# Hybrid decoder layer on one core: the down projection in seven products per pair, with its sums formed during the up projection and kept in DRAM

## The chip, the core and the metric

The kernel runs on one core of one Trainium2 chip. The metric is the device time of one execution in microseconds (us). TensorE (PE) multiplies matrices into PSUM; VectorE (DVE), ScalarE (ACT) and GpSimd (POOL) work elementwise; SyncE (SP) issues most of the DMA transfers. Each engine works through its own queue in order and waits on semaphores of the others.

## The reference, cut to what matters

One layer of a decoder for 1024 tokens of width 1024, all in float32. A token-mixing half (attention in windows of 128 in parallel with a gated linear recurrence, then an output projection) is followed by a squared-ReLU MLP with 4096 hidden columns. The change touches the MLP alone:

```python
h = rmsnorm(x, pre_w_mlp[l]) * (1.0 + sc2) + sh2
u = jnp.square(jax.nn.relu(h @ w_up[l]))
x = x + g2 * rmsnorm(u @ w_down[l], post_w_mlp[l])
```

`w_up` is 1024x4096 and `w_down` is 4096x1024; `g2` comes from the conditioning vector through a slice of the matrix called `wada` in the kernel.

## The kernel before, in words

**Precision.** Every big matrix product is made in float32 from two reduced-precision halves: an operand is split into `hi` (a rounding copy on ACT) and `lo` (operand minus `hi`, on DVE), and the product is hi x hi + hi x lo + lo x hi. So one 128x128 by 128x512 block product is three matmuls, and every operand block that comes from DRAM costs one ACT and one DVE instruction of 128x512 before TensorE can use it.

**The up projection** (from line 1159 on; the loop over `p` is at line 1178). The 32 blocks of 128 hidden columns are taken in 16 pairs. The first four blocks (pairs 0 and 1, "CL") are done in the plain way by `up_cl`. For pairs 2 to 15 the product of a 2x2 arrangement (two hidden blocks by two halves of the inner dimension, against two halves of the inner dimension by two halves of the tokens) is made by Strassen's scheme in its Winograd form: seven products instead of eight, each of 12 matmuls. The token side's sums (`bt`, numbers 1 to 8, `factors` at line 994) are formed once and stay in SBUF; the weight side's sums are formed for each pair by `up_weights` (line 1041: four DVE sums, seven splits). `prod` (line 1064) issues the 12 matmuls of one product, and `up_pair` (line 1096) puts products 1, 4 (of the pair before), 5, 2, 6, 3, 7 in order. They accumulate in three PSUM banks, called `pua`, `puc`, `pub` in the profile. Between products a bank is copied out by ACT (`snap`) or added to an SBUF tile by DVE (`merge`). `act2` (line 1086) then applies ReLU on ACT and the square on POOL, and POOL issues the DMA that writes the block to the DRAM tensor `ud`. The tiles of these results (`s1`, `s5`, `s2`, `u`) come from a pool `poolM` of 16 buffers, eight of which hold the sums number 4 of the token side. Weights are loaded one to two pairs ahead by `up_loads` on SP, through pools of four (`poolR2`) and three (`poolR`) buffers.

**The down projection** (`down`, line 1199) is plain. In eight stages `s` of four hidden blocks, for each of eight token blocks `tb` and both halves of the output columns, 12 matmuls go into a fresh PSUM bank (`pd` in the profile, from a pool `pb` of five banks), and DVE adds the bank to an SBUF accumulator `acc`. While a stage runs, `load_u` and `load_wd` fetch the next stage's operands from DRAM (`ud` and `w_dn`, 16 blocks of 128x512 in a stage) on SP and split them on ACT and DVE. In stages 2 to 5 the vector `gw2` (`g2` times the output norm's weight) is computed by `modrow` (line 161): 16 loads of `wada` and 16 multiply-adds `macc` on DVE. In the last stage each token block, once finished, is normalised, scaled, added to the residual `x1` (reloaded from DRAM) and stored (`final`, line 1228); the last two blocks have code of their own (`last_two`, line 1236).

**What sets the order.** The program's text gives the order of dependences; a scheduler then places the instructions on each engine's queue by its own estimate of when they become ready, except where the text pins engines to program order (`pin`). Pools hand out buffers, and an instruction that writes a buffer waits until all readers of its former content, DMA writes among them, are done. All engine instructions go through the helper class at line 39, so profile rows name tiles rather than lines.

Of the kernel before, what the change touches and what calls it, by code (L numbers as in the profile page):

```python
# [16 lines left out]
P = 128  # L17
# [30 lines left out]
def hybrid_layer(ctx: ExitStack, tc: tile.TileContext, I, out, dbg=None):  # L48
# [963 lines left out]
    ud = dram.tile([2 * NG, 2, P, 512], F32, tag="ud", name="ud")  # L1012
# [28 lines left out]
    def up_weights(p, ns=(1, 5, 2, 6, 3, 7, 4)):  # L1041
        for n in ns:
            a11, a12, a21, a22 = (araw[p, k] for k in ("a11", "a12", "a21", "a22"))
            if n == 5:
                araw[p, "s1"] = s1 = t_(f"s1_{p}")
                DVE.tensor_tensor(s1, a21, a22, ALU.add)
                wsplit(5, p, s1)
            elif n == 6:
                araw[p, "s2"] = s2 = t_(f"s2_{p}")
                DVE.tensor_tensor(s2, araw[p, "s1"], a11, ALU.subtract)  # L1050
                wsplit(6, p, s2)
            elif n == 3:
                s4 = t_(f"s4_{p}")
                DVE.tensor_tensor(s4, a12, araw[p, "s2"], ALU.subtract)
                wsplit(3, p, s4)
# [30 lines left out]
    def act2(p, src, f, th, e=None, on_act=False):  # L1086
# [7 lines left out]
        nc.gpsimd.dma_start(ud[2 * p + f, th], e)  # L1094

    def up_pair(p):
        if (p, "a") not in banks:
            prod(p, 1)
        if (p - 1, "a") in banks:
            prod(p - 1, 4, False)  # L1100
            act2(p - 1, banks[p - 1, "a"], 1, 0)
# [5 lines left out]
        act2(p, ev[p, "s1"], 0, 0, ev[p, "s1"])  # L1107
# [10 lines left out]
    NS, SF = 8, 4  # L1118
    us, wd = {}, {}
    DPn = {}  # L1120

    def d_(name, dt=F32):
        return DPn["d"].tile([P, 512], dt, tag="d", name=name)

    def load_u(s, th, raws_=None, mk=None):
        for i, f in enumerate(range(SF * s, SF * s + SF)):
            rk = raws_[i % len(raws_)] if raws_ else raw_
            us[f, th] = split(load_raw(rk, f"ur{f}_{th}", ud[f, th]), mk or (d_ if th == 1 and f % SF else m_), f"u{f}_{th}")

    def load_wd(s, half, raws_=None):  # L1130
        for i, f in enumerate(range(SF * s, SF * s + SF)):
            rk = raws_[i % len(raws_)] if raws_ else raw_
            wd[f, half] = split(load_raw(rk, f"wdr{f}_{half}", I["w_dn"][f][:, half * 512:half * 512 + 512]),
                                hT_, f"wd{f}_{half}")
# [10 lines left out]
    def up_cl(f, th):  # L1145
# [4 lines left out]
        act2(f // 2, pst, f % 2, th, t_(f"rl{f}_{th}"), True)  # L1150
# [12 lines left out]
    R2 = uctx.enter_context(tc.tile_pool(name="poolR2", bufs=4))  # L1163
    load_cl(3)
# [12 lines left out]
    up_loads(p0 + 1)  # L1177
    for p in range(p0, NG):
        if p + 1 < NG:
            up_weights(p + 1, (1, 5, 2))  # L1180
        else:
            pin(True, SP)
            load_wd(0, 0, (raw_, t_))
            load_u(0, 0, (raw_, t_), hT_)
            load_wd(0, 1, (raw_, t_))
            pin(False, SP)
# [5 lines left out]
    prod(NG - 1, 4, False)  # L1192
    act2(NG - 1, banks[NG - 1, "a"], 1, 0)
    uctx.close()
    DPn["d"] = ctx.enter_context(tc.tile_pool(name="poolD", bufs=12))

    accs = [[None, None] for _ in range(TB)]

    def down(s, tb):
        sl = slice(tb % 4 * P, tb % 4 * P + P)  # L1200
        fs = range(SF * s, SF * s + SF)
        for half in range(2):
            pst = tp_ps(f"pd{s}_{tb}_{half}")
            proj3(pst, [tuple(u[:, sl] for u in us[f, tb // 4]) for f in fs], [wd[f, half] for f in fs])
            if s == 0:
                accs[tb][half] = g_(f"acc{tb}_{half}")
                ACT.activation(accs[tb][half], pst, AF.Copy)
            else:
                DVE.tensor_tensor(accs[tb][half], pst, accs[tb][half], ALU.add)
# [26 lines left out]
    def last_two(s, x16, x17):  # L1236
        a, b = TB - 2, TB - 1
        pin(True, ACT, DVE, POOL, PE)
        down(s, a)
        fs = range(SF * s, SF * s + SF)  # L1240
        lhs = [tuple(u[:, 3 * P:] for u in us[f, 1]) for f in fs]
        ss = small.tile([P, 3], F32, tag="ssl", bufs=1, name="ssl")
        one = {n: small.tile([P, 1], F32, tag="l_" + n, bufs=1, name="l_" + n) for n in ("part", "t", "r")}
        finl = a_ps("finl")
        cols = ((0, 512), (512, 768), (768, D))
        accl = [accs[b][c0 // 512][:, c0 % 512:c0 % 512 + c1 - c0] for c0, c1 in cols]

        def piece(n):
            c0, c1 = cols[n]
            pst = tp_ps(f"pdl{n}")[:, 0:c1 - c0]  # L1250
            half, b0 = c0 // 512, c0 % 512
            proj3(pst, lhs, [tuple(w[:, b0:b0 + c1 - c0] for w in wd[f, half]) for f in fs])
            DVE.tensor_tensor(accl[n], pst, accl[n], ALU.add)
            ACT.activation(finl[:, 0:c1 - c0], accl[n], AF.Square, accum_out=ss[:, n:n + 1])

        def gate(n):
            DVE.tensor_tensor(accl[n], accl[n], gw2[:, cols[n][0]:cols[n][1]], ALU.mult)

# [115 lines left out]
```

## Time and profile before

| | |
|---|---|
| median of 3 runs | 1166.39 us (1164.28 to 1167.32) |
| the profiled execution | 1165.2 us, its span from first to last instruction 1163.4 us |
| PE / DVE / ACT / POOL busy | 1116.1 / 690.2 / 497.6 / 315.4 us |
| DMA over the span | 132.82 MB |
| up projection, pairs 2 to 15 | about 533 to 802 us |
| down projection | 802 to 1151 us |

A group row of the profile reads: line, engine, operation, out<-in by the program's names, shape, count | busy us, mean ns of one | idle time of the engine before them and what ended it. A row of the chain of waits reads: start, length (us), what, how many instructions. A row of the timeline reads: start, length, engine, instruction, and in brackets the idle time before it with what ended that. A window row gives the busy time of each engine in a stretch with the number of instructions, then the granted clock, the busy share of the 16 DMA engines and the GB/s moved.

### The profile page before, as it was taken

Reading aid. Unit: us, or ns where it says so; the run is one execution under the profiler, and the core shown is the slowest. Engines: PE = TensorE matmul, PEld = TensorE weight load, DVE = VectorE, ACT = ScalarE, POOL = GpSimd, SP = SyncE. Lnnn points to the kernel's source line nnn. Section 1 sums busy time; section 2 is a strip of 40 time slices with the busy share of each in tenths; the row PEclk is TensorE's granted clock in tenths of the full one; section 3 lists DMA queues with packets and bytes.
Section 4 is the critical chain, followed back from the end, with each engine's and each line's share of the span. In section 5 each row is a group of like instructions: output and inputs, shape, how many; then the busy total and the mean of one; then the engine's idle time right before and its main releaser. Section 6 shows DMA issues by size and latency. Waiting matters only on the chain.

```text
span 1163.4 us, 15657 instructions
## 1 busy us (share of the span) xinstructions
PE 1116.1 (96%) x5590; PEld 914.3 (79%) x5590; DVE 690.2 (59%) x1181; ACT 497.6 (43%) x1064; POOL 315.4 (27%) x432
## 2 busy tenths in 40 slices
PE   3899999999999999999999999999999999999995
PEld 3778776788788788878788888888888888888884
DVE  4875777878765565479554545447545454454445
ACT  5454644364555655556444444435522221221122
POOL 3444221043235544422333333332000000000053
PEclk9899999999999999999999999999999999999998
DMA  9700400534311422413323323237624342333133
GB/s 336 256 10 3 144 1 22 189 98 139 110 55 44 150 106 91 150 68 104 124 106 111 117 103 123 83 118 255 216 82 127 100 124 94 99 121 98 46 109 136
DMA packets 68607, 132.82 MB, mean 114 GB/s; under 512 B 9264, under 2 KB 10032, under 8 KB 68528
## 3 DMA queue, kind: packets, MB, share of 16 engines
q1 hardware_dynamic: 61200, 108.21, 28.1%
q0 software_dynamic: 7040, 23.07, 5.1%
q8 instruction: 44, 0.72, 0.2%
q10 hardware_dynamic: 288, 0.52, 0.1%
q14 instruction: 35, 0.29, 0.1%
HBM read 106.61 MB, written 25.17 MB: 113 GB/s over the span
## 4 chain that ended last, share of the span: by engine, by line
PE 79%; DVE 7%; ACT 4%; POOL 3%; DMA 2%; issue 2%; DVEq 0%; SPq 0%; POOLq 0%; ACTq 0%
PE pd L39 29%; PE pua L39 12%; PE po L39 6%; PE puc L39 6%; PE pu L39 4%; PE pub L39 3%; PE pv L39 3%; PE pq L39 2%; PE phg L39 2%; PE phq L39 2%; PE phf L39 2%; DVE m L39 1%; PE pk L39 1%; PE sc L39 1%; PE oT L39 1%
## 5 line engine op out<-in xcount | busy, mean ns | idle before, releaser
L39 DVE TENSOR_TENSOR acc<-pd,acc 128x512 f32<-128x512 f32 x110 | 74.8, 687 | 60.6 <-PE pd L39 60.6
L39 POOL TENSOR_TENSOR s<-s 128x512 f32<-128x512 f32 x42 | 48.6, 1156 | 126.0 <-ACT s L39 126.0
L39 DVE TENSOR_TENSOR wt<-s,wt 128x512 fp32r<-128x512 f32 x42 | 29.0, 692 | 65.9 <-ACT wt L39 65.9
L39 ACT ACTIVATE wt<-a 128x512 fp32r<-128x512 f32 x56 | 35.0, 629 | 50.2 <-PE pub L39 18.6
L39 DVE TENSOR_TENSOR wt<-a,wt 128x512 fp32r<-128x512 f32 x56 | 39.2, 700 | 28.1 <-ACT wt L39 28.1
L39 DVE SCALAR_TENSOR_TENSOR macc<-wada,cs,macc 128x512 f32<-128x512 f32 x56 | 44.9, 802 | 11.9 <-DMA wada<-wada 11.2
L39 PE MATMUL pd<-wd_0l,u_0h 128*128 128x512 f32 x128 | 49.8, 389 | 0.0
L39 PE MATMUL pd<-wd_0h,u_0l 128*128 128x512 f32 x128 | 49.8, 389 | 0.0
L39 PE MATMUL pd<-wd_1h,u_0h 128*128 128x512 f32 x128 | 49.8, 389 | 0.0
L39 PE MATMUL pd<-wd_1l,u_0h 128*128 128x512 f32 x128 | 49.8, 389 | 0.0
L39 PE MATMUL pd<-wd_1h,u_0l 128*128 128x512 f32 x128 | 49.8, 389 | 0.0
L39 PE MATMUL pd<-wd_0h,u_0h 128*128 128x512 f32 x128 | 49.8, 389 | 0.0
L39 ACT ACTIVATE u_1h<-ur 128x512 fp32r<-128x512 f32 x32 | 20.0, 628 | 66.8 <-DMA ur<-ud 66.8
L39 PE MATMUL pd<-wd_0h,u_1h 128*128 128x512 f32 x124 | 48.2, 389 | 0.0
L39 PE MATMUL pd<-wd_0l,u_1h 128*128 128x512 f32 x124 | 48.2, 389 | 0.0
L39 PE MATMUL pd<-wd_0h,u_1l 128*128 128x512 f32 x124 | 48.2, 389 | 0.0
L39 PE MATMUL pd<-wd_1h,u_1h 128*128 128x512 f32 x124 | 48.2, 389 | 0.0
L39 PE MATMUL pd<-wd_1l,u_1h 128*128 128x512 f32 x124 | 48.2, 389 | 0.0
L39 PE MATMUL pd<-wd_1h,u_1l 128*128 128x512 f32 x124 | 48.2, 389 | 0.0
L39 ACT ACTIVATE wd_0h<-wdr 128x512 fp32r<-128x512 f32 x32 | 20.1, 631 | 63.4 <-PE pd L39 33.0
L39 PE MATMUL pua<-bt_0h,wt 128*128 128x512 f32 x112 | 43.8, 391 | 1.5 <-DVE s L39 1.5
L39 DVE TENSOR_TENSOR u_1l<-ur,u_1h 128x512 fp32r<-128x512 f32 x32 | 22.0, 691 | 37.0 <-ACT u_1h L39 37.0
(624 smaller groups left out, 3428.0 us busy)
## 6 DMA issues: line engine op xcount, KB each, us to landing
wada<-wada SPq DMA_DIRECT2D x64, 256.0 KB, 3.2
wdr<-w_dn SPq DMA_DIRECT2D x64, 256.0 KB, 2.9
ur<-ud SPq DMA_DIRECT2D x64, 256.0 KB, 2.7
a<-w_u SPq DMA_DIRECT2D x56, 256.0 KB, 2.8
ud<-s POOLq DMA_DIRECT2D x42, 256.0 KB, 2.7
wa<-wada SPq DMA_DIRECT2D x32, 256.0 KB, 5.2
x<-x SPq DMA_DIRECT2D x16, 256.0 KB, 4.9
xr<-x SPq DMA_DIRECT2D x16, 256.0 KB, 2.9
```

The lines of the kernel that those rows point to most:

```text
L39: ins = op(*args, **kw)
```

## The change

The down projection goes over to the same seven-product scheme, with blocks of hidden pairs as inner dimension, the two halves of the tokens on one side and the two halves of the output columns on the other.

- Up phase, activations: after the four squared blocks of a pair (`a11`, `a12`, `a21`, `a22`) DVE forms four sums of them (`usum`, numbers 7, 5, 6, 3), and seven blocks instead of four are written to `ud`. The square moves from POOL to ACT. The pairs 0 and 1 get their sums by POOL from blocks reloaded from DRAM (`direct_sums`).
- Up phase, weights: `down_sums` loads the four blocks of `w_dn` of one pair through a new pool `poolB` of three buffers, POOL forms four differences, and POOL's queue writes them to a new DRAM tensor `td`. One pair's sums are issued per iteration, from pair 0 on; in iterations 4, 5 the direct sums and in 11, 13 the last two pairs' weight sums come on top.
- `gw2` (`modrow`) moves from the down phase into iterations 6 to 9 of the up phase.
- In `up_weights` the three sums share one buffer.
- Down phase: the 16 pairs are taken in five groups (4, 4, 3, 3, 2 pairs). For the first four groups, for each of the seven products (`dstage`), four token blocks get 3 matmuls for each pair of the group into a bank, after which `accum` adds the bank to an accumulator. Product 1 starts a bank "a" which products 6, 7 and 4 continue; product 5 starts a bank "c" which 3 continues; product 2 has a bank "b". The two sets of four banks change roles from group to group. `dprep` loads and splits a product's operands up to 16 pairs ahead. In the last group the loop is turned round: `drows` does all seven products for one token block of each half, so that two token blocks are finished together; `last_rows` is the last of these, pinned.

The instructions on POOL between the up phase's results of pair 7 and pair 8. In these rows `ud` is the activations' DRAM tensor, `td` the weight sums', `b..` the blocks of `w_dn`, `us..`, `s..` and `u..` results of the pair named by their first number. Before:

```order
L39 TENSOR_TENSOR s1_8_6392<-s1_8_6392 128x512
L1094 DMA ud_5005<-s1_8_6392 128x512
L39 TENSOR_TENSOR s2_8_6438<-s2_8_6438 128x512
L1094 DMA ud_5005<-s2_8_6438 128x512
L39 TENSOR_TENSOR s5_8_6407<-s5_8_6407 128x512
L1094 DMA ud_5005<-s5_8_6407 128x512
L39 TENSOR_TENSOR u_8_10_6533<-u_8_10_6533 128x512
L1094 DMA ud_5005<-u_8_10_6533 128x512
```

Now the queue holds, for about half a pair:

```order
L1097 DMA ud_5005<-s5_7_6474 128x512
L1104 DMA ud_5005<-s2_7_6505 128x512
L1104 DMA ud_5005<-us2_7_6543 128x512
L39 TENSOR_TENSOR b11_9_7126<-b22_9_7130,b11_9_7126 128x512
L1147 DMA td_5006<-b11_9_7126 128x512
L39 TENSOR_TENSOR b22_9_7130<-b22_9_7130,b10_9_7124 128x512
L1147 DMA td_5006<-b22_9_7130 128x512
L1097 DMA ud_5005<-u_7_10_6651 128x512
L1104 DMA ud_5005<-us4_7_6655 128x512
L39 TENSOR_TENSOR b21_9_7136<-b21_9_7136,b22_9_7130 128x512
L1147 DMA td_5006<-b21_9_7136 128x512
```

The writes of the activations stand between subtractions and writes of weight sums; the scheduler has put the weight sums earlier than the program's text (the sums of pair 9 stand among pair 7's results). Between the first `us3` write of a pair and that of the next stand 5 to 8 subtractions and 12 to 15 DMA issues for the pairs 3 to 11, and 7 to 9 DMA issues with no more than 2 subtractions from pair 12 on.

The end of the first row block of the last group on PE. `pda4_0` is bank "a" of token blocks 0 and 4, `pda4_1` that of 1 and 5; the first number behind `dw` and `du` is the pair, the second the product. Before, two fresh banks simply follow each other (the last matmuls of one, the first of the next):

```order
L39 MATMUL pd7_4_1_10133<-wd31_1h_9687,u31_1h_9663 128x512
L39 MATMUL pd7_4_1_10133<-wd31_1l_9688,u31_1h_9663 128x512
L39 MATMUL pd7_4_1_10133<-wd31_1h_9687,u31_1l_9664 128x512
L39 MATMUL pd7_5_0_10168<-wd28_0h_9621,u28_1h_9645 128x512
L39 MATMUL pd7_5_0_10168<-wd28_0l_9622,u28_1h_9645 128x512
L39 MATMUL pd7_5_0_10168<-wd28_0h_9621,u28_1l_9646 128x512
```

Now product 7 continues bank "a", four matmuls of the next row block's product 1 follow, and then product 4 continues the same bank "a":

```order
L39 MATMUL pda4_0_10605<-dw15_7_10526,du15_7h_10531 128x512 x2
L39 MATMUL pda4_0_10605<-dw15_7_10526,du15_7l_10532 128x512
L39 MATMUL pda4_1_10699<-dw14_1h_10274,du14_1h_10280 128x512
L39 MATMUL pda4_1_10699<-dw14_1l_10275,du14_1h_10280 128x512
L39 MATMUL pda4_1_10699<-dw14_1h_10274,du14_1l_10281 128x512
L39 MATMUL pda4_1_10699<-dw15_1h_10286,du15_1h_10292 128x512
L39 MATMUL pda4_0_10605<-dw14_4_10577,du14_4h_10582 128x512 x2
L39 MATMUL pda4_0_10605<-dw14_4_10577,du14_4l_10583 128x512
```

So DVE's read of the bank after product 7 has to fit into four matmuls.

The diff, cut to its core:

```diff
@@ up phase @@
-    ud = dram.tile([2 * NG, 2, P, 512], F32, tag="ud", name="ud")
+    ud = dram.tile([NG, 8, P, 512], F32, tag="ud", name="ud")
+    td = dram.tile([NG, 8, P, 512], F32, tag="td", name="td")
+    ux = dram.tile([CL // 2, P, 512], F32, tag="ux", name="ux")
+    FAC = {(0, 0): 1, (1, 0): 2, (1, 1): 4}
...
-        if on_act:
-            ACT.activation(e, e, AF.Square)
-        else:
-            POOL.tensor_tensor(e, e, e, ALU.mult)
-        nc.gpsimd.dma_start(ud[2 * p + f, th], e)
+        ACT.activation(e, e, AF.Square)
+        if (f, th) in FAC:
+            nc.gpsimd.dma_start(ud[p, FAC[f, th]], e)
+        elif p < CL // 2:
+            nc.gpsimd.dma_start(ux[p], e)
+        return e
+
+    def usum(p, n, dst, x, y, op, eng=None):
+        (eng or DVE).tensor_tensor(dst, x, y, op)
+        nc.gpsimd.dma_start(ud[p, n], dst)
+        return dst
...
+    def last_of(p):
+        prod(p, 4, False)
+        a12 = act2(p, banks[p, "a"], 1, 0)
+        usum(p, 3, m_(f"us4_{p}"), a12, us2.pop(p), ALU.subtract)
...
-        act2(p, ev[p, "s2"], 0, 1, ev[p, "s2"])
+        a21 = act2(p, ev[p, "s2"], 0, 1, ev[p, "s2"])
+        usum(p, 7, m_(f"us3_{p}"), a11, a21, ALU.subtract)
         prod(p, 7, False)
         merge(p, "a", "s5")
-        act2(p, ev[p, "s5"], 1, 1, ev[p, "s5"])
+        a22 = act2(p, ev[p, "s5"], 1, 1, ev[p, "s5"])
+        s1 = usum(p, 5, a21, a21, a22, ALU.add)
+        us2[p] = usum(p, 6, m_(f"us2_{p}"), s1, a11, ALU.subtract)
...
+        def put(n, t, x, y):
+            POOL.tensor_tensor(t, x, y, ALU.subtract)
+            nc.gpsimd.dma_start(td[p, n], t)
...
@@ down phase @@
+    GROUPS = [range(0, 4), range(4, 8), range(8, 11), range(11, 14), range(14, 16)]
+    stages = [(g, n) for g in range(4) for n in (1, 5, 6, 3, 7, 2, 4)] + [(4, n) for n in (1, 5, 2, 6, 3, 7, 4)]
...
+    PLAN = {1: ("a", True, 0, 0), 5: ("c", True, 1, 1), 6: ("a", False, 0, 1), 3: ("c", False, 0, 1),
+            7: ("a", False, 1, 1), 2: ("b", True, 0, 0), 4: ("a", False, 1, 0)}
...
+    def dstage(g, n):
+
+        key, first, th, half = PLAN[n]
+        for t in range(4):
+            if first:
+                mks = ([tp_ps] * 4, [tp_ps, mm_ps, mm_ps, a_ps])[(g + (key != "a")) % 2]
+                dbank[key, t] = mks[t](f"pd{key}{g}_{t}")
+            dmm(dbank[key, t], g, n, t, first)
+            accum(t + 4 * th, half, dbank[key, t])
...
-    for s in range(NS - 1):
-        for i in range(2):
-            load_u(s + 1, i)
-            load_wd(s + 1, i)
...
+    for i, (g, n) in enumerate(stages[:-7]):
+        dprep_upto(i)
+        dstage(g, n)
+    dprep_upto(len(stages) - 7)
+    x1 = [x1_load(0), x1_load(4)]
+    for t in range(3):
+        drows(4, t)
...
+    last_rows(4, *x1)
```

More of the change, by code (lines that the diff above doesn't have):

```diff
@@ L1137, in hybrid_layer, with dprep_upto @@
+    dnext = [0]
+    def dprep_upto(i):
+        while dnext[0] < len(stages) and sum(len(GROUPS[g]) for g, _ in stages[i:dnext[0] + 1]) <= 16:
+            dprep(dnext[0])
+            dnext[0] += 1
     cw = {}
@@ L1211, in x1_load, with drows @@
+    def drows(g, t):
+        bk = {}
+        for _, n in stages[-7:]:
+            key, first, th, half = PLAN[n]
+            if first:
+                bk[key] = (mm_ps if key == "a" else tp_ps)(f"pd{key}{g}_{t}")
+            dmm(bk[key], g, n, t, first)
+            accum(t + 4 * th, half, bk[key])
     def x1_load(tb):
```

226 lines of the change are left out of this document (135 added, 91 removed).

## The prediction

> **What bounds the kernel now.** I read the page's busy shares first, then the windows of the two phases that change, then the chain of waits, then the groups of POOL, DVE and ACT that the edits touch, and last the timeline around their dependences. The busy line, and one window from each phase:
>
> ```profile
> PE 1116.1 (96%) x5590; PEld 914.3 (79%) x5590; DVE 690.2 (59%) x1181; ACT 497.6 (43%) x1064; POOL 315.4 (27%) x432
> ...
> 600.00:700.00 100.00, 100.00 (x443) 82.81 (x442) 51.14 (x74) 43.70 (x74) 35.47 (x42) 1.00 0.31 111
> ...
> 900.00:1000.00 100.00, 100.00 (x443) 82.80 (x442) 50.16 (x76) 23.15 (x38) 2.22 (x2) 1.00 0.34 106
> ```
>
> In both phases TensorE is busy all the time at clock 1.00, the others half of it or less. The chain of waits says the same: one pair of the up phase, then the whole down phase.
>
> ```profile
> 719.75 8.16 PE pua L39 x36
> 727.91 2.72 PE puc L39 x12
> 730.63 2.72 PE pub L39 x12
> 733.35 2.72 PE pua L39 x12
> 736.07 2.72 PE puc L39 x12
> 738.79 8.16 PE pua L39 x36
> ...
> 802.47 129.65 PE pd L39 x572
> 932.58 87.04 PE pd L39 x384
> 1020.07 114.25 PE pd L39 x504
> ```
>
> A product of 12 matmuls takes 2.72 us, so a matmul 0.2267 (87.04/384 too), and a pair recurs every 738.79 - 719.75 = 19.04 us. Only fewer matmuls, or a new wait, can move this stretch.
>
> **The matmuls.** The down projection has 8 stages x 8 token blocks x 2 halves x 12 = 1536 matmuls of 128x512. Changed it has 16 pairs x 7 products x 4 token blocks x 3 = 1344. Saved: 192 x 0.2267 = **43.5 us**, all of it on the path. The rest is what the new work costs where it is not hidden.
>
> **Up phase, ACT and DVE.** The rows:
>
> ```profile
> L39 POOL TENSOR_TENSOR s<-s 128x512 f32<-128x512 f32 x42 | 48.6, 1156 | 126.0 <-ACT s L39 126.0
> L39 ACT ACTIVATE s<-s 128x512 f32<-128x512 f32 x42 | 26.5, 632 | 23.4 <-DVE s L39 21.5
> L39 DVE TENSOR_TENSOR wt<-a,wt 128x512 fp32r<-128x512 f32 x56 | 39.2, 700 | 28.1 <-ACT wt L39 28.1
> L39 DVE SCALAR_TENSOR_TENSOR macc<-wada,cs,macc 128x512 f32<-128x512 f32 x56 | 44.9, 802 | 11.9 <-DMA wada<-wada 11.2
> ```
>
> ACT gets four squares for each pair, 4 x 0.63 = 2.5 us on top of 44% of 19.04 = 8.4: 10.9, or 57%. DVE gets four sums, 4 x 0.70 = 2.8 on top of 51% = 9.7: 12.5, or 66%. Both stay below the pair's 19.04, so their bare time costs nothing; TensorE's cover would be gone only above 6 us more. In the two iterations with `modrow` DVE has 8 x 0.80 + 2 x 0.70 = 7.8 more, 20.3 us in all, 1.3 over; I charge 1.5 us for each of the two, since the merges wait behind the `macc` on DVE's queue, the ReLUs for the merges and product 7 for the copy on ACT behind them. Together 3 us (0 to 6).
>
> **Up phase, POOL.** This is the engine that fills up. POOL loses its squares and gets two-input subtractions and many more DMA issues.
>
> ```profile
> L1094 POOL DMA_DIRECT2D ud<-s x42 | 24.4, 580 | 12.5 <-POOL s L39 12.5
> L39 POOL TENSOR_TENSOR acc<-acc,x 128x512 f32<-128x512 f32 x9 | 13.2, 1483 | 3.5 <-DVE acc L39 3.5
> ...
> 664.53 1.34 POOL L39 TENSOR_TENSOR s<-s 128x512 f32<-128x512 f32 x1 [3.88 <-ACT s L39]
> 666.17 0.58 POOL L1094 DMA_DIRECT2D ud<-s  x1 [0.30 <-POOL s L39]
> 667.78 1.03 POOL L39 TENSOR_TENSOR s<-s 128x512 f32<-128x512 f32 x1 [1.03 <-ACT s L39]
> ...
> 664.29 0.68 DVE L39 TENSOR_TENSOR s<-a,s 128x512 f32<-128x512 f32 x1
> 664.89 1.53 DVE L39 TENSOR_TENSOR a<-a,a 128x512 f32<-128x512 f32 x1
> 666.34 0.68 DVE L39 TENSOR_TENSOR s<-pua,s 128x512 f32<-128x512 f32 x1
> ```
>
> An issue takes 0.58, and 0.30 more of idle time where it follows POOL's own result. An elementwise operation takes 1.03 alone and 1.34 to 1.48 beside DVE; and in the last rows a DVE operation with two SBUF inputs that starts while POOL's is running takes 1.53 instead of 0.68, whereas its neighbour with a PSUM input does not stretch. The Trainium skill has the rule behind this row (GPSIMD Engine Reference, "8. Key points"): POOL shares its SBUF interfaces with VectorE and contends with DVE instructions that have two SBUF inputs. The trace agrees (1.53 against 0.68), and the rule speaks against this change, which adds such operations on both engines.
>
> By the order of the changed program POOL has, between the first `us3` write of pair 3 and that of pair 11, 53 subtractions and 109 issues; TensorE needs 8 x 19.04 = 152.3 us for these eight pairs. Low: 53 x (1.03 + 0.30) + 109 x 0.58 = 133.7. High: 53 x 1.48 + 109 x (0.58 + 0.30) = 174.4. Middle, an operation at 1.2 with the 0.30 behind it: 53 x 1.5 + 109 x 0.58 = 142.7. So POOL takes 88% to 115% of TensorE's time there, most likely 94%. A late POOL reaches TensorE only through buffers: a tile written out by POOL's queue is free when the write has landed.
>
> ```profile
> ud<-s POOLq DMA_DIRECT2D x42, 256.0 KB, 2.7
> ```
>
> For instance `a22`: product 7 ends at 722.47 in the pair above, a merge (0.69), ReLU and square (0.63 each) make it 724.4, issue and landing (0.58 + 2.7) 727.7; if the eight free buffers go round in turn, its buffer is wanted by the copy after product 6 of the next pair, at 736.07. So some 8 us of lag are free. The high case lags 22 us and would cost 14; the middle none. I take 2 us (0 to 14), nearer to the middle since the 1.03 row is the commoner.
>
> **Up phase, transfers.** A pair now moves 8 loads and 11 writes of 256 KB, 5.0 MB in 19.04 us or 262 GB/s, against 111 in the window above. In the eight crowded pairs the order holds 96 loads and 109 writes, 53.7 MB in 152.3 us or 353 GB/s. What the queues can carry is shown at the kernel's start:
>
> ```profile
> 15.00:20.00 5.00, 3.71 (x18) 3.49 (x18) 3.96 (x14) 2.67 (x5) 0.17 (x1) 1.00 1.05 406
> ```
>
> 406 GB/s is above 353, so I charge 1 us for later landings (0 to 4). A page of the Trainium skill gives less room (DMA: Bandwidth & Descriptors, "Specifications"): about 358 GB/s from HBM for a core. The trace disagrees with it for this kernel, 406 on one core; by the page's figure the crowded stretch would be 99% full and the sum some 5 us longer, an estimate.
>
> **Border of the phases.** It shows one stall of TensorE today:
>
> ```profile
> PE pua L39 <- DVE s L39: 1.5, 1, 1.5
> ```
>
> Now four matmuls of the first down stage stand ahead of the last product 4, which may hide it, but twice as many splits of the first stages stand on ACT and DVE. I take +1 us (-1.5 to +4).
>
> **Down phase, the first four groups.** Loads: 224 blocks instead of 128, 58.7 MB in 305 us, 193 GB/s, under 406. DVE: 224 splits instead of 128 and some 140 evictions (16 of them on ACT) instead of 128.
>
> ```profile
> L39 DVE TENSOR_TENSOR acc<-pd,acc 128x512 f32<-128x512 f32 x110 | 74.8, 687 | 60.6 <-PE pd L39 60.6
> L39 DVE SCALAR_TENSOR_TENSOR acc<-acc,r_f,gw 128x512 f32<-128x512 f32 x12 | 8.5, 749 | 12.4 <-POOL r_f L39 12.4
> ```
>
> A stage of a three-pair group costs DVE 6 x 0.70 + 4 x 0.69 = 7.0 us of TensorE's 36 x 0.2267 = 8.16; of a four-pair group 8.4 of 10.88. A bank is read again by TensorE a whole stage later at the earliest, so DVE's read is hidden; POOL is idle there. Cost 0 (0 to 4).
>
> **The last group.** Here TensorE waits, I think. A product is 6 matmuls, 1.36 us. Bank "a" after product 6 must be read before product 7, 1.36 us later, and after 7 before 4, four matmuls or 0.91 us later. How long a read takes after the last matmul:
>
> ```profile
> 1106.72 0.39 PE L39 MATMUL pd<-wd_1h,u_1l 128*128 128x512 f32 x1
> 1106.95 0.39 PE L39 MATMUL pd<-wd_0h,u_0h 128*128 128x512 f32 x1
> ...
> 1107.15 0.69 DVE L39 TENSOR_TENSOR acc<-pd,acc 128x512 f32<-128x512 f32 x1 [2.03 <-PE pd L39]
> ```
>
> The next slot begins at 1106.95 and the read ends at 1107.84: 0.89 us. It just fits, if DVE is free. It seldom is: in the last 4 x 9.52 = 38.1 us it has about 30 additions (20.6 us), 12 scalings (9.0), 7 sums with `x1` (4.8), and the end's two products and two scalings (2.9), 37 in all; and a scaling waits for POOL's `r_f`, which now stands behind two `x1` sums of 1.48 each for the other row block. I expect about 1.5 us of wait in each of the last three row blocks, **4.5 us** (1 to 10). The end behind the last matmul keeps its form (addition, square, root on POOL, scaling, store): 0 (-1 to +1).
>
> **Sum.** Against the profiled execution of 1165.2 us (span 1163.4, 1.8 around it): 1165.2 - 43.5 + 3 + 2 + 1 + 1 + 0 + 4.5 = **1133.2 us**. The runs' median, 1166.39, lies 1.2 (0.1%) above this execution; 0.3%, 3.5 us, is about what a measurement of this kernel can tell from no change, so I leave the difference out.
>
> **The rivals.**
> *POOL sets the pace of the crowded pairs* (chance 0.17). With the high prices it costs 14 us where 2 are charged, and late `b` loads on SP, which stand ahead of the next weights' loads, can add the 4 of the transfers' bound where 1 is charged: 1145 to 1148 us. For: every price's high end stands in a row, and 34 transfers in the pairs with `modrow` (8.9 MB) need 22 us at 406 GB/s. Against: the pairs from 12 on have nearly no subtractions.
> *DVE sets the pace of the down phase* (0.05). If its operations took 0.82 as `macc` does, a three-pair stage would need 8.2 us of 8.16 and no late read would be made up for: with 0.5 to 0.75 us of wait in each of the 28 stages of the first four groups, 1147 to 1154 us. For: DVE goes from half busy to 86% of such a stage. Against: POOL, which stretches DVE's operations, stands still there.
> *The gain is given back whole* (0.02): all terms at their high ends together, 6 + 14 + 4 + 4 + 4 + 10 + 1 = 43 us, 1165 us.
> *Slower: the ring of result buffers* (0.06). A pair's copies out of PSUM wait for tiles whose writes POOL has not issued, because POOL itself waits for a `b` load, and SP can issue that one only when POOL's former write out of the same three buffers has landed: a loop through two queues. Its pace depends on landings, and those stretch when the queues are full:
>
> ```profile
> wa<-wada SPq DMA_DIRECT2D x32, 256.0 KB, 5.2
> ```
>
> Each us of lag beyond the free 8 is paid once in each of the ten crowded pairs. Of the gain 34 us are left after the other charges (43.5 - 9.5), used up at 3.4 us for each pair, a lag of 11.4; at a lag of 13 it comes to 1131 + 50 = some 1181 us. For: 5.2 against 2.7 is the landing under load, twice in each turn of the loop. Against: the scheduler has spread the `b` work over earlier pairs, and the middle price leaves POOL 6% free.
> That the change does not do what it says is excluded: the order holds the 1344.
>
> **How the numbers follow.** The forecast's own range has 0.70: low ends 1165.2 - 43.5 + 1 - 1.5 - 1 = 1120.2, and up to about 1142, where the first rival begins. With the first two rivals the range reaches 1120 to 1154. Faster by over 0.3%: 0.70 + 0.17 + 0.05 = 0.92; within 0.3%: 0.02; slower: 0.06.
>
> **What would show it.** Right: pairs still recur at 19.04 us in the chain; 2.72 us per 12 matmuls; TensorE waits for `acc` on DVE in the last 38 us and little elsewhere; POOL busy about nine tenths from pair 3 to 11. Wrong: pairs at 20 us or more with TensorE waiting for `s` on ACT, whose wait ends with a DMA write (the ring) or on POOL; gaps between `pd` stages; or a last group without waits.

## The result and the profile after

The changed kernel takes **1229.45 us** (median of 4 runs, 1224.99 to 1239.84) against 1166.82 of the kernel before (4 runs): a ratio of 1.055, with a 95% interval of 1.049 to 1.062. It is slower by 63 us, where 33 us less were forecast. The profiled execution has a span of 1227.0 us.

The page's first lines after. The forty slices are 30.7 us each; the dent from slice 18 to 30 is the up phase.

```profile
PE 1106.2 (90%) x5392; PEld 895.7 (73%) x5392; DVE 832.0 (68%) x1347; ACT 575.0 (47%) x1216; POOL 410.6 (33%) x560
...
PE   4899999999999999977877788689989999999994
...
PEclk9899999999999999989898998889989999999997
```

The windows of the two phases: up to the last product of the up phase (in after its last 4 us fall into the second window), and from there to the end of the matmuls (in after these end at 1213.97, 4 us ahead of the window's end). First of after, then of before:

```profile
533.00:897.00 364.00, 293.27 (x1173) 234.27 (x1172) 236.40 (x298) 159.57 (x276) 184.50 (x232) 0.91 0.68 230
897.00:1218.00 321.00, 310.68 (x1354) 255.17 (x1353) 228.04 (x359) 135.82 (x262) 23.61 (x38) 0.98 0.60 194
```

```profile
533.00:802.00 269.00, 267.48 (x1179) 220.79 (x1178) 146.49 (x213) 122.38 (x210) 94.47 (x111) 1.00 0.34 120
802.00:1151.00 349.00, 348.78 (x1551) 289.09 (x1549) 175.87 (x265) 91.99 (x166) 26.18 (x38) 1.00 0.37 119
```

The down phase went from 349 to 321 us, or to some 317 without the empty 4 us. All of the loss, 95 us by the windows, is in the up phase: the same matmuls (1173 and 1179) took 364 us where they took 269. There TensorE stands 364 - 293 = 71 us, and its matmuls run at a granted clock of 0.91. At 0.2267 us each, 1173 matmuls are 266 us; so 98 us are lost, 71 by standing and 27 by the clock.

What it stands for, and what VectorE and SyncE's queue stand for in the same stretch of after (us in total, times, longest):

```profile
PE pua L39 <- DVE s L39: 47.4, 11, 9.3
PE pua L39 <- ACT s L39: 14.6, 4, 4.4
PE pua L39 <- DVE wt L39: 6.4, 1, 6.4
```

```profile
DVE s L39 <- DMA a<-w_u: 44.4, 11, 8.1
DVE wt L39 <- ACT wt L39: 42.6, 29, 3.4
DVE macc L39 <- DMA wada<-wada: 14.1, 6, 3.7
```

```profile
SPq L39 <- DMA td<-b: 124.7, 43, 6.9
SPq L39 <- DVE wt L39: 51.5, 19, 12.0
SPq L39 <- POOL b L39: 46.2, 21, 6.6
```

TensorE waits for bank "a" to be copied or merged (`s`); VectorE waits for the blocks of the next weights (`a`, from `w_u`); and SyncE waits for writes of weight sums (`td`) to land, because the next `b` load goes into their buffer. One scene of after shows the three in a row, SyncE, VectorE, TensorE:

```profile
633.54 0.33 SPq L39 DMA_DIRECT2D b<-w_dn  x1
633.98 0.85 SPq L39 DMA_DIRECT2D a<-w_u  x2
```

```profile
639.79 1.55 DVE L39 TENSOR_TENSOR s<-a,a 128x512 f32<-128x512 f32 x1 [4.54 <-DMA a<-w_u]
641.37 0.69 DVE L39 TENSOR_TENSOR a<-a,a 128x512 f32<-128x512 f32 x1
641.98 0.68 DVE L39 TENSOR_TENSOR s<-puc,s 128x512 f32<-128x512 f32 x1
642.58 0.68 DVE L39 TENSOR_TENSOR wt<-a,wt 128x512 fp32r<-128x512 f32 x1
646.45 0.49 DVE L39 TENSOR_SCALAR macc<-wada,cs 128x512 f32<-128x512 f32 x1 [3.19 <-DMA wada<-wada]
646.85 0.68 DVE L39 TENSOR_TENSOR us<-s,s 128x512 f32<-128x512 f32 x1
647.46 0.68 DVE L39 TENSOR_TENSOR s<-pua,s 128x512 f32<-128x512 f32 x1
```

```profile
648.19 0.79 PE L39 MATMUL pua<-bt_0h,wt 128*128 128x512 f32 x1 [6.80 <-DVE s L39]
648.79 0.63 PE L39 MATMUL pua<-bt_0l,wt 128*128 128x512 f32 x1
649.21 0.63 PE L39 MATMUL pua<-bt_0h,wt 128*128 128x512 f32 x1
```

The two `a` loads are issued at 633.98, right behind a `b` load in front of which SyncE had stood for some 4 us. VectorE, which takes its instructions in order, stands 4.54 us for such an `a`, later 3.19 for a load of the gate's row, and only then comes to the merge `s<-pua` that TensorE needs; TensorE has stood 6.80 us by then. After the stop its matmuls follow each other at 0.43 us (648.79 to 649.21) and not at 0.2267.

The other thing seen is VectorE's time for the same instruction. The weight split, first of after, then of before:

```profile
L39 DVE TENSOR_TENSOR wt<-s,wt 128x512 fp32r<-128x512 f32 x42 | 41.9, 998 | 26.1 <-ACT wt L39 24.7
```

```profile
L39 DVE TENSOR_TENSOR wt<-s,wt 128x512 fp32r<-128x512 f32 x42 | 29.0, 692 | 65.9 <-ACT wt L39 65.9
```

In the last group TensorE waits 6.3 us in four places for additions on VectorE (`pdla` 3.4, `pda` 1.9, `pdlx` 1.0), close to the 4.5 forecast.

### The profile page after: what moved, and what is told of

Read it like the earlier page. It is cut to its first block, busy times and chain, and to the rows that moved or that the text cites. A ratio compares the mean times of both kernels' runs of the same rounds, so it can differ in the third digit from the quotient of the medians.

```text
span 1227.0 us, 16242 instructions
## 1 busy us (share of the span) xinstructions
PE 1106.2 (90%) x5392; PEld 895.7 (73%) x5392; DVE 832.0 (68%) x1347; ACT 575.0 (47%) x1216; POOL 410.6 (33%) x560
## 5 line engine op out<-in xcount | busy, mean ns | idle before, releaser
L39 POOL TENSOR_TENSOR b<-b,b 128x512 f32<-128x512 f32 x64 | 91.2, 1426 | 88.9 <-DMA b<-w_dn 84.0
L39 PE MATMUL pua<-bt_0h,wt 128*128 128x512 f32 x112 | 50.5, 450 | 69.1 <-DVE s L39 47.4
L39 ACT ACTIVATE s<-s 128x512 f32<-128x512 f32 x84 | 52.9, 630 | 92.9 <-DVE s L39 91.5
L39 ACT ACTIVATE wt<-s 128x512 fp32r<-128x512 f32 x42 | 26.5, 631 | 81.8 <-DVE s L39 45.7
L39 DVE TENSOR_TENSOR acc<-pda,acc 128x512 f32<-128x512 f32 x64 | 43.7, 687 | 28.6 <-PE pda L39 28.0
L39 DVE TENSOR_TENSOR dw<-dwr,dw 128x512 fp32r<-128x512 f32 x72 | 48.4, 684 | 12.3 <-ACT dw L39 12.3
L39 PE MATMUL pua<-bt_1h,wt 128*128 128x512 f32 x112 | 49.2, 439 | 0.0
L39 PE MATMUL pua<-bt_2h,wt 128*128 128x512 f32 x112 | 48.8, 436 | 0.0
L39 ACT ACTIVATE dw<-dwr 128x512 fp32r<-128x512 f32 x72 | 43.0, 620 | 10.8 <-PE pua L39 4.7
L39 PE MATMUL pua<-bt_3h,wt 128*128 128x512 f32 x112 | 46.4, 416 | 0.0
L39 DVE TENSOR_TENSOR s<-a,a 128x512 f32<-128x512 f32 x14 | 13.8, 987 | 44.4 <-DMA a<-w_u 44.4
L1147 POOL DMA_DIRECT2D td<-b x64 | 35.6, 556 | 16.9 <-POOL b L39 16.9
```

Of the source, the lines that this page charges most:

```text
L39: ins = op(*args, **kw)
L1147: nc.gpsimd.dma_start(td[p, n], t)
```

## The experiments

Four theories stood at the start. **Queue theory:** SyncE, in front of a `b` load whose buffer is still being written out, keeps the loads of the next weights behind it. **Transfer theory:** the 16 DMA engines are too full and everything lands late. **Port theory:** GpSimd's subtractions stretch VectorE's instructions. **Sums theory:** the sums of the activations on VectorE and the squares on ScalarE are too much. Unless a text says otherwise, a kernel is the changed one with the edit shown and ran once, with a profile; the run of the kernel before on the same chip gave 1170.2 (first four), 1163.7, 1164.9, 1167.2 and 1165 us. The changed kernel's own runs spread over 15 us, so differences of a few us between single runs say nothing.

| kernel | us | kernel | us |
|---|---|---|---|
| changed | 1229.5 | e10 product order | 1224.4 |
| e3 no subtraction | 1206.9 | e11 = e7 + order | 1212.9 |
| e4 no weight sums | 1145.2 | e12 = e4 + order | 1147.6 |
| e5 SyncE in text order | 1218.3 | e13 = e11 + sums on VectorE | 1180.3 |
| e6 no `td` writes | 1201.9 | e16 sums on VectorE | 1199.2 |
| e1 `b` loads on GpSimd | 1250.9 | e15 = e7 + `a` loads first | 1212.7 |
| e7 more `b` buffers | 1211.8 | e14 = e15 + sums on VectorE | 1193.4 |
| e8 = e1 + e7 | 1219.3 | e17 gate's row in down phase | 1248.8 |
| e9 = e4 + 64 idle subtractions | 1185.5 | e18 shared-out buffers | 1196.4 |
| | | e20 two queues by hand | 1193.4 |

**What of the weight sums costs.** Three kernels leave parts out; e5 holds SyncE to the order of the text.

```
e3  def put:  -            POOL.tensor_tensor(t, x, y, ALU.subtract)
e6  def put:  -            nc.gpsimd.dma_start(td[p, n], t)
e4            -        down_sums(p - p0)          (and its two entries in JOBS)
e5            +    pin(True, SP)                  (ahead of the loop over p)
```

> The blocks of w_dn are still loaded into the ring of three buffers and written out to td, but GpSimd's subtraction between is left out (the output is then not the reference's). Port theory (GpSimd's two-input subtractions stretch VectorE's own two-input instructions, 998 ns against 692 before for a weight split, and this alone makes weights late): the up phase goes back from 365 us to about 270, the total from 1229 to about 1135. Queue theory (SyncE stands in front of a b load until a former td write has landed, 124.7 us of such waits in the up phase, and the next weights' loads stand behind it): those waits stay, since loads and writes stay; a gain of 10 to 35 us only, for the 1.4 us that each subtraction adds to a buffer's round. Transfer theory (16 DMA engines too full): no change, within 5 us. Sums theory (VectorE's and ScalarE's added sums and squares of the up result are too much): no change, within 5 us.

> No weight sums at all: no b load in the up phase but the eight of the two clear pairs, no subtraction, no td write; the down phase loads a plain w_dn block where it would load a sum (the output is then not the reference's). Queue, transfer and port theories all say that the weight sums are the whole of the loss: the up phase back at 265 to 280 us and the total at 1128 to 1145. Sums theory (VectorE's four-operation sums of the up result and ScalarE's squares alone overfill a pair): the up phase stays over 320 us and the total over 1185. In between, both have a share: the difference to 270 us is the share of the sums of the up result, their writes, and the gate's row in this phase.

> Only the order of SyncE's queue in the up phase changes: it is held to the order of the program text, so that a pair's b loads come first, then the rest, and the a loads of pair p+2 stand behind all of them. Queue theory: the loss depends on what stands behind which b load, so the time must move by 15 us or more, and TensorE's waits for s with it; down if the a loads come to stand where their b loads have all been let go (total 1150 to 1210), up if not. Transfer, port and sums theories: the same bytes and instructions, so within 8 us of 1229.

> The b loads and GpSimd's subtractions stay, only the writes of the sums to td are left out (the down phase loads plain w_dn blocks in their place, so the output is not the reference's). A b buffer then comes free when its subtraction ends, not when a write has landed. Queue theory: SyncE's 124.7 us of waits for td writes go, and of the 95 us of loss at least 60: total 1130 to 1170. Transfer theory: 4 of about 19 transfers of a pair go, so a fifth to a third of the loss, total 1195 to 1215. Port theory: the subtractions stay, so 1215 to 1235. Sums theory: within 5 us of 1229.

e4 clears the activations' sums and the squares: without weight sums the kernel takes 1145.2, so the weight sums are 84 us of the loss. Its windows show the rest: 196, 420 and 198 matmuls in 500 to 550, 600 to 700 and 800 to 850 us, where before has 231, 443 and 222. At 0.2267 us the missing 35, 23 and 24 are 7.9, 5.2 and 5.4 us: a wait at the phase's start, the gate's row, and the border. Leaving out the subtractions (e3) gives 23 us, which the queue theory had expected (10 to 35); leaving out the writes (e6) gives 28, which the transfer theory had expected (1195 to 1215) and the queue theory had not (at least 60); SyncE's order (e5) gives 11, between what the theories said and close to the spread of the runs. None of the parts is the cause alone. e4 leaves the sums theory aside; these kernels do not tell the other three apart. In e6 SyncE no longer waits for `td`, but 116.4 us for GpSimd's subtractions to free the buffers: the wait had only changed its name.

**Queue and port apart.** In e1 and e8 the `b` loads go to GpSimd's queue; e7 gives half of them buffers of `poolT`; e9 tests the port without any `b` load.

```
e1  -        b22 = load_raw(b_, f"b22_{p}", ...)     e7  -        b21 = load_raw(b_, ...)
    +        b22 = load_b(f"b22_{p}", ...)               +        b21 = load_raw(t_, ...)
e9  +        d = b_(f"dm{p}")
    +        POOL.memset(d, 1.0)
    +        for k in range(4):
    +            POOL.tensor_tensor(d, d, d, ALU.subtract)
```

> The loads of the w_dn blocks for the sums are issued from GpSimd's own queue instead of SyncE's; same bytes, same subtractions, same three buffers. Queue theory (SyncE's queue, standing in front of a b load, keeps the next weights' a loads behind it): the a loads are free, VectorE's waits for them (44 us in the up phase) fall under 10; total 1150 to 1190, or, if GpSimd now stands itself in front of b loads with the result writes behind it, the waits of ScalarE and VectorE for M buffers grow and up to half of the gain goes. Transfer theory and port theory: nothing that they count changes, 1220 to 1235.

> Two of a pair's four b loads (b11 and b21 of the scheme) take their buffer from the five buffers of poolT, of which the up phase now uses only one per pair; the other two keep the three of poolB. So no b load stands behind a write of its own pair any more; bytes, instructions and queues are unchanged. Queue theory: SyncE's waits for td writes (124.7 us) fall under 40 and the total to 1145 to 1185. Transfer theory: unchanged or worse, 1220 to 1240. Port theory: unchanged, 1215 to 1235.

> Both edits: b loads on GpSimd's queue, and two of four in poolT's buffers. Queue theory: the best of the three, 1140 to 1175, since neither queue stands long; what is left above the 1145 of the kernel without weight sums is the price of the transfers and of GpSimd's subtractions. If the port theory or the transfer theory holds for a larger part, it stays over 1190.

> Measures the port by itself: the kernel without weight sums (1145.2 us), but GpSimd does 64 subtractions on a buffer of its own (and 16 fills), with no load and no write for them (the down phase loads plain w_dn blocks, so the output is not the reference's). Port theory: VectorE's two-input instructions are stretched and the up phase is as slow as in the changed kernel: 1190 to 1230. Queue and transfer theories: no queue is touched and no byte is added, so 1143 to 1155; what it is above 1145 is the price of the subtractions.

e1 came out slower than every theory had said. Its rows of the up phase show why. GpSimd waits for `b` loads to land as long as in the changed kernel (78.7 us there), and now it also stands in front of the loads themselves until their buffer has been written out; the results' writes stand behind both, and ScalarE waits for result tiles (0.4 us in the changed kernel):

```profile
POOL b L39 <- DMA b<-w_dn: 79.4, 35, 6.0
POOL b L1145 <- DMA td<-b: 17.4, 11, 3.3
```

```profile
ACT s L39 <- DMA ud<-us: 34.3, 7, 11.8
```

e7 gained 18 us, less than expected; 82 us of waits for `td` stayed. e8, with both edits, is no better (1219.3). And e9 was the surprise: 64 subtractions (and 16 fills) that nobody waits for, with no byte moved and no load added, cost 40 us on top of e4. Its timeline shows how, GpSimd first:

```profile
634.08 6.02 POOL L39 TENSOR_TENSOR dm<-dm 128x512 f32<-128x512 f32 x6
```

```profile
633.69 0.68 DVE L39 TENSOR_TENSOR s<-pua,s 128x512 f32<-128x512 f32 x1
634.29 6.37 DVE L39 TENSOR_TENSOR wt<-a,wt 128x512 fp32r<-128x512 f32 x1
```

A weight split of 0.68 us took 6.37: it started 0.2 us after GpSimd's first of six subtractions and ended after the last. The neighbour, with a PSUM input, took its 0.68. ScalarE waits for the write of a result tile only once in e9's up phase (3.0 us), so GpSimd's late queue is not what costs here. So the port is a cause of its own, and in this scene a run of subtractions held VectorE for the whole run. The Trainium skill (SBUF — State Buffer, "Who interferes with whom") has a VectorE instruction with two SBUF inputs contend with a GpSimd instruction that reads SBUF, and calls contention for the shared ports an exclusive lock. The trace agrees: the split ended 0.56 us after the last subtraction, as if it had only been let in then; but it was blocked over six of GpSimd's instructions, not over one.

**Does lead on TensorE's side help?** If VectorE is only sometimes late, more products between two uses of bank "a" would hide it.

```
-            prod(p - 1, 4, False)    -> 1, 4', 5, 2, 6, 3, 7
+    order of prod in up_pair         -> 1, 5, 4', 6, 2, 3, 7   (4' = of the pair before)
```

> The changed kernel with only the order of the products in the up phase altered: 1, 5, 4 of the pair before, 6, 2, 3, 7 in place of 1, 4 of the pair before, 5, 2, 6, 3, 7, so that between two products into bank a, where ScalarE's copy or VectorE's merge has to come between, there are always two other products (5.4 us) and not one (2.7 us). Lead theory (each delay of VectorE, whether by a late load or by GpSimd's subtractions, is paid by TensorE as far as it goes over the one product that lies between): a large part of the 84 us comes back, total 1150 to 1195, and TensorE's waits for s (62 us) fall under 25. Throughput theory (VectorE or the queues are simply behind, pair after pair, so lead only shifts the wait): 1215 to 1240.

> The new order of products, and two of four b loads in poolT's buffers (that alone gave 1211.8). Lead theory with queue theory: 1135 to 1170. If lead does not help: 1205 to 1220.

> The new order of products without any weight sums (the old order gave 1145.2; the output is not the reference's). Lead theory: the waits for s of that run (some 7 us) go too, 1134 to 1143; what is left above 1132 is the start of the phase, the gate's row and the border to the down phase. If the order costs something by itself (ScalarE's copies now come close together), 1145 to 1160.

> As the new order with poolT's buffers, but the 64 subtractions of weight blocks on VectorE (0.68 us each, 43.5 us more in the up phase) and none on GpSimd. Port theory: GpSimd's subtractions cost VectorE more than its own would (each holds it up for as long as 1.3 us), so this is faster than the same kernel with GpSimd's, by 3 to 20 us. Without a port effect VectorE only has more to do and more loads to stand before: slower by 5 to 30 us.

The lead theory fell: -5, +1 and +2 us. That fits a VectorE that is behind pair after pair, so that lead only moves the wait. e13 was the largest step so far: the 64 subtractions on VectorE itself, 43.6 us more work for it, made the kernel 33 us faster than e11.

**Each cause without the other.**

```
e16 def put:  -            POOL.tensor_tensor(t, x, y, ALU.subtract)
              +            DVE.tensor_tensor(t, x, y, ALU.subtract)
e15 +    pin(True, SP)     +        up_loads(p + 2, ("a11", "a12", "a21"))   ahead of the b loads
```

> The changed kernel, only the 64 subtractions of weight blocks moved from GpSimd to VectorE; loads, buffers and product order as changed. Port theory as a cause by itself: 1185 to 1205 (it gave 32 us on top of the other edits). If it only counts where the queue no longer stands (the two hide each other): 1215 to 1235; if the queue gets worse because VectorE in order now waits for b loads too: over 1235.

> SyncE's queue is held to the program's order, written so that three of the four a loads of pair p+2 come ahead of all b loads of iteration p, the fourth right after the weights that free its buffer, and four b loads come in each iteration in three portions (two to four in the two iterations with the clear pairs' sums); two of four b loads in poolT's buffers; subtractions on GpSimd. Queue theory: VectorE no longer waits for a loads (31 us before, under 8 now) and what is left is the port's: 1165 to 1195. If the queue was not what was left: 1205 to 1220, as without the order (1211.8).

> The same with the subtractions on VectorE. If queue and port are the two causes and there is no third: 1140 to 1160, near the 1145 of the kernel without weight sums. If VectorE is then too full or stands before b loads: 1165 to 1185.

The port counts by itself: e16 gave 30 us. With e7's 18 that makes 48, and both together (e13) gave 49: two causes that add. But with the subtractions on VectorE the loads stand in its way directly. Of e16, then of e14:

```profile
DVE b L39 <- DMA b<-w_dn: 59.2, 30, 5.8
```

```profile
DVE b L39 <- DMA b<-w_dn: 39.4, 24, 5.9
DVE s L39 <- DMA a<-w_u: 13.9, 9, 3.7
```

e15 and e14 missed: `a` loads ahead of `b` loads on SyncE did not help. I put that down to `a22`, which still had only a pair and a half of buffers: SyncE now stood 108 us (e15) and 104 us (e14) for VectorE to be done with weights (51.5 in the changed kernel), with the `b` loads behind.

**Is VectorE's work the pace?** In the slow kernels VectorE hardly ever waits for TensorE, so I took work from it that has nothing to do with the sums.

```
e17 up loop:    -            m5 = modrow(5, (p - 6) // 2, t_, "b_g2", "postw2", gw2)
    down loop:  +        if i in (9, 16):
                +            for _ in modrow(5, i // 16, t_, "b_g2", "postw2", gw2): pass
e18 = e17, put on DVE, a12/a22/b21 from t_, s1/b11 from raw_, a21 from r2_
```

> The changed kernel, only the final gate's row (two times 8 loads, 8 VectorE operations of 0.75 us and a split) moved from the up phase back to the down phase. In the up phase it held VectorE for 14 us of waits for its loads and some 12 us of work. If VectorE sets the pace of every pair: 15 to 26 us come back, total 1203 to 1214. If it does not: no more than the 3 us of the forecast or the 5 that the kernel without weight sums lost in these pairs, 1222 to 1231.

> The gate's row in the down phase, the 64 subtractions on VectorE, and the buffers shared out anew so that no load stands behind its own pair: a12, a22 and b21 from poolT, s1 and b11 of the scheme from poolR, a11 and a21 from poolR2. VectorE's work is then some 14.3 us of a pair's 19.04 (12.8 in the kernel without weight sums, less 1.3 for the row, plus 2.75). If VectorE's own time and its waits for loads are the whole cause: 1130 to 1150, faster than before. If the transfers are a cause of their own, since they stay (landings of 4 to 5 us), 1155 to 1185.

e17 came out 19 us slower, the wrong way, which speaks against the theory that VectorE's work sets the pace. It is no clean test of it, since the scheduler also ordered SyncE's queue anew (the phase starts with five `b` loads in a row, where the changed kernel has three); in the up phase of e17 SyncE stands longer than in the changed kernel (164.2 us against 124.7), and VectorE with it (71.7 against 44.4):

```profile
SPq L39 <- DMA td<-b: 164.2, 44, 5.9
```

```profile
DVE s L39 <- DMA a<-w_u: 71.7, 11, 14.0
```

e18 (4 runs, 1188.0 to 1197.9; ratio to before 1.025, 1.020 to 1.029) missed both its 1130 to 1150 and the 1155 to 1185 of the transfers: SyncE still waited 109.7 us for `td` and VectorE 27.4 and 23.1 us for `b` and `a`. What stands in front of what was still the scheduler's choice, so the last kernel writes that by hand.

```
+    pin(True, SP, DVE)
     for p in range(p0, NG):
+        up_loads(p + 2)                       # all four a blocks, a pair and more ahead
+        ds = down_sums(p - p0); next(ds)      # three b loads; sums later, between the merges
...
+        w(6)                                  # inside up_pair: weights of the next pair
+        next(ds)                              # one sum
+        merge(p, "b", "s1")
```

> Both in-order queues are written out by hand in the up phase: SyncE loads all four a blocks of pair p+2 and three b blocks at the start of iteration p (the fourth b block after the first sum), VectorE forms the weights of pair p+1 and four weight sums between the merges, at least 8 us behind the loads. Sums on VectorE, the gate's row and the weight sums of the last two pairs in the down phase, buffers as in e18_best. If what stands in front of what is the rest of the cause: VectorE's waits for a and b loads fall under 10 us, total 1135 to 1165. If the transfers themselves or VectorE's load are the rest: the waits move to another place and it stays at 1175 to 1200.

The total missed again: 1193.4 (4 runs, 1192.9 to 1197.2; ratio to before 1.025, 1.023 to 1.027). By the total alone the transfers or VectorE's load would be the rest (1175 to 1200). But its windows say what the total does not. From 700 to 800 us, first of e20, then of after, then of before:

```profile
700.00:800.00 100.00, 100.00 (x440) 81.87 (x439) 72.61 (x116) 53.61 (x96) 30.06 (x56) 1.00 0.74 256
```

```profile
700.00:800.00 100.00, 78.59 (x303) 62.92 (x304) 64.84 (x77) 38.05 (x66) 59.00 (x74) 0.87 0.71 241
```

```profile
700.00:800.00 100.00, 100.00 (x443) 82.57 (x441) 51.12 (x73) 44.83 (x77) 34.93 (x42) 1.00 0.34 123
```

With four weight sums formed in every pair, all their loads and writes made (256 GB/s, more than after's 241) and VectorE at 73% (after 65%, before 51%), TensorE does 440 matmuls in 100 us, as good as before's 443. So neither the bytes nor the work is too much. That it is the order shows beside e18, whose sums, port and buffers are the same; it differs in the order of the two queues, and in that e20 forms the last two pairs' sums later:

```profile
700.00:750.00 50.00, 41.17 (x170) 33.25 (x169) 30.75 (x50) 21.16 (x37) 13.62 (x26) 0.90 0.73 257
750.00:800.00 50.00, 43.60 (x180) 35.16 (x179) 32.74 (x52) 22.62 (x40) 15.57 (x29) 0.93 0.75 260
```

With as many bytes e18 does 350 matmuls where e20 does 440. In both SyncE stands some 50 us of the 100 for `td` writes (47.2 and 50.9). But e18's queue holds five `b` loads in a row with `a` loads behind them, and VectorE waits 14.8 us for `a` and 7.9 for `b`; e20's has the four `a` loads of a pair ahead of its `b` loads, and VectorE waits for neither. What e20 still loses is in few stops of TensorE (from 500 to 1160 us):

```profile
PE puc L39 <- ACT s L39: 29.5, 2, 15.5
PE pmodb_g L39 <- DVE acc L39: 14.6, 2, 14.3
```

The first two stops lie in the iterations with the clear pairs' sums, where I had put five loads `x..` ahead of the fourth `b` load on SyncE; VectorE, pinned, stood for that block with a sum of the next weights behind it; ScalarE stood 19.69 us for that sum with the copy of bank "c" behind it, and TensorE 15.47 us for the copy:

```profile
602.75 0.32 SPq L39 DMA_DIRECT2D xd<-ud  x1
606.74 0.32 SPq L39 DMA_DIRECT2D xe<-ud  x1
611.03 0.32 SPq L39 DMA_DIRECT2D xb<-ud  x1
611.41 0.42 SPq L39 DMA_DIRECT2D b<-w_dn  x1
```

```profile
615.69 0.69 DVE L39 TENSOR_TENSOR b<-b,b 128x512 f32<-128x512 f32 x1 [21.14 <-DMA b<-w_dn]
```

The other is the gate's row in the down phase: its matmul waits for additions on VectorE, which by the releaser free its bank. Without these 44 us e20's profiled 1193.5 would be some 1149 us, below before. That is an estimate; such a kernel was not run.

## Why the prediction was wrong

- **Matmuls saved, 43.5 us: right.** 192 matmuls fewer, and in the down phase TensorE runs without a gap up to the last group (50.00 of 50 us and 220 to 223 matmuls in every window from 900 to 1150). The phase is 28 us shorter by the windows, 32 without the 4 us behind the last matmul; most of the rest of the 43.5 is the last group's waits, 6.3 us, and matmuls that run slow behind a stop, nearly 4 (1354 of them are busy for 310.7 us, 307 at 0.2267).
- **Last group, 4.5 us: right in kind and nearly in size** (6.3). **First four groups, 0: right.** **Gate's row, 3, and border, 1:** e4 gives 5.2 and 5.4; the wait of 6.4 us for `wt` at the start of the phase was not in the sum.
- **"Both stay below the pair's 19.04, so their bare time costs nothing": this step failed.** I had the row with 1.53 us in the text and a rule that spoke against the change, and then costed VectorE at 0.70 for each instruction. GpSimd's 64 subtractions took VectorE's splits from 692 to 998 ns (706 in e16); leaving them out gave 23 us (e3), moving them to VectorE 30 (e16), and alone they cost 40 (e9, in longer runs than in the changed kernel).
- **Transfers, "406 GB/s is above 353, so I charge 1 us": this step failed too, and by what is left of the 84 us it was the larger part: 44 to 61, an estimate from the 23 to 40 of the subtractions.** It priced the queues by their bytes. The landings did grow only a little (`a` 4.1 us in the median against 2.7), and 256 GB/s went beside a full TensorE in e20. What counted was the order in one queue: a `b` load that cannot start holds up the weights' loads behind it. I had written that down, as "late `b` loads on SP, which stand ahead of the next weights' loads", and allowed it 4 us; it is part of those 44 to 61.
- **GpSimd, 2 us through the result buffers: wrong way in.** GpSimd is busy 184.5 of 364 us, not nine tenths, since the pairs grew longer with it. In the changed kernel ScalarE's copies wait for such a tile once, 0.4 us.
- **The rival "ring of result buffers" (1181 us)** had the loop right, GpSimd waiting for a `b` load (78.7 us) and SyncE for the write before it (124.7), but led it to TensorE through the result tiles. That path shows in e1 alone (34.3 us), and the sign named for it, TensorE waiting for `s` on ScalarE, is 14.6 us of the 71 against 47.4 on VectorE. The real one leads through the weights: SyncE, `a` load, VectorE in order, merge, TensorE.
- **The rival "POOL sets the pace"** was wrong in its price: beside the subtractions it let VectorE go on. No rival came near 1229 us.
- **The clock** was in no term: of the 98 us, 27 are matmuls that run slow after a stop.

What the runs leave open: how the 84 us divide in the changed kernel itself (port 30 and buffers 18 add up; that the order of the two queues clears the rest, with the sums on VectorE, shows from 700 to 800 us of e20 and not in its total), and whether GpSimd's subtractions could be hidden with that order too. Both were not tried.

## What to carry to other kernels

Before moving loads into a phase, write down for each in-order queue what stands behind the new instruction and when its buffer comes free; a share of bandwidth or of busy time does not show it. Where a VectorE instruction that TensorE needs within a product's time stands behind one that waits for a fresh load, the load's latency is TensorE's. And two-input work on GpSimd is not free for VectorE: here the kernel was 30 us faster when VectorE did the 64 subtractions itself, at 0.69 us each.

## What the runs showed of the hardware

- A VectorE instruction with two SBUF inputs can be held over several GpSimd instructions in a row: 6.37 us for 0.68 (e9).
- A long stop of TensorE costs more than itself: after 6.80 us without work the matmuls came at 0.43 us for some 3 us; over the 18 stops of the up phase that makes 27 us, 1.5 for each on average. A short stop costs no more than itself: after 0.81 us, in the last group, they came at some 0.23. The Trainium skill (TensorE: Matmul & The Clock Gate, "Part 1: The HAM clock gate") has TensorE at half its clock after an idle window of about 3.4 us until it has been busy for one; the rows of the long stop agree (0.43 against 0.2267, for some 3 us).
- DMA traffic of 256 GB/s beside a full TensorE cost it nothing (e20, 700 to 800 us), while the changed kernel lost a third of its matmuls there at 241 (303 of 443).
